# Rotary tables turned once and repeated through DRAM, a parity mask spread by loads: one change to a hybrid decoder block

## Chip, core and metric

The kernel runs on one core of a Trainium2 chip. The metric is the device time of one execution in microseconds; the figure that counts is the median over several runs of the whole kernel.

## What is computed

The reference is a decoder block on 1024 positions of width 1024, in float32. Two of its parts matter here: the rotary embedding of q and k, and the masked attention of three head groups.

```python
def apply_partial_rope(t, cos, sin):          # first 16 of 64 dims of each head
    t1, t2 = rot[..., :half], rot[..., half:] # half = 8
    rotated = concatenate([t1 * cos - t2 * sin, t1 * sin + t2 * cos])

def reference(x, positions, ...):
    inv_freq = ROPE_THETA ** (-arange(0, ROT_DIM, 2) / ROT_DIM)   # 8 frequencies
    ang = positions[..., None] * inv_freq                         # 1024 x 8
    cos, sin = cos(ang), sin(ang)
    h = rms_norm(x, mix_norm_g)
    z_a, q, k, v, gate_logits = split(h @ w_in)
    y_a = chunked_spatial_gating(gelu(z_a), ...)
    q, k = apply_partial_rope(q, cos, sin), apply_partial_rope(k, cos, sin)
    y_b = dilated_mixture_attention(q, k, v)   # groups (128,1), (512,4), (2048,16)
    merged = sigmoid(g_A) * (y_a @ w_branch_a) + sigmoid(g_B) * (y_b @ w_branch_b)
    x = x + merged @ w_out
    ...                                        # norm, convolutional gated MLP, final norm
```

The third attention group, number 2, has dilation 16. The kernel handles it in eight tiles of 128 positions that interleave two residues, so a query may see a key only if both have the same parity in the tile and the key is not later: its mask is a parity mask with a causal one on top.

## The kernel before

**Tiles and order.** All big products are float32 products split in high and low parts, with the transposed activations as moving operand and weights as stationary one. The stage in which the change lies is the input projection `h @ w_in`. It goes by pairs of 256 output columns; each pair is seven products P1 to P7 (a Strassen-like scheme), and each product is 12 matmuls of 128x128 by 128x512 into one PSUM bank (`in_product`, L534). The list `in_order` (L327) fixes the order; the loop over it (L1385) has index i. Pairs 0 and 1 are done ahead; pair 2 is the last of the zv columns, pairs 3, 4, 5 are q/k (rotated dims), q/k (other dims) and v of attention group 1, pairs 6 to 8 the same of group 2, 9 to 11 of group 0. Index i = 7 ends pair 2, i = 8 to 13 are the rest of pair 3, i = 14 to 20 pair 4, i = 21 on pair 5.

**Who sets the order.** TensorE (PE) runs in program order throughout. VectorE (DVE) and ScalarE (ACT) run in program order up to i = 18 (`ordered`, L1379 to L1400); from then on, and for SyncE (SP, which issues nearly all DMAs) and GpSimd (POOL) everywhere, a planner at build time orders each engine's instructions by when it thinks that their inputs are there. On the chip each engine then takes its own list strictly in order. An instruction written later in the program but free to move can be placed between ordered ones.

**Work hung on the matmuls.** After each sixth matmul of a product `tick()` (L216) runs; `after(n, fn)` puts fn on the n-th tick from now, so two ticks are one product. Beside i = 13 to 20 run `norm_v` and `spatial(b)`, b = 0 to 7, one `spatial` at the end of each of these products (L713): 24 small matmuls into two PSUM tiles `pm`, then six passes on DVE (L738) that read them, then stores to DRAM (`mixd`, L743). Both `pm` tiles come from `ps_tr`, a pool of two banks (`tr_tile`, L154). `in_ahead(i, 9, 4)` (L334) loads weights nine places ahead into five buffers `wr` and splits operands four places ahead (ACT L313 the high part, DVE L314 the low one). `sums_ahead` makes the sums that two of the operands need (DVE L278 to L280).

**The rotary tables.** `rot_tables` (L2459) works in `lent`, the part of a buffer `swap` that is free until the first q/k pair is ready. A chain of small DVE steps reduces the angles of 128 positions by 64 (8 blocks of positions by 8 frequencies); `sines` (L2513) makes the two 128x64 tables `sn` and `cs` on ACT. The rotation needs them the other way round, in `YC`: two tables of 128 rows by 1024 positions, where the rows repeat the 8 frequencies four times for each of four heads, with the sign of half the sine rows turned. To get there, `widen` (L2519, 16 ACT passes of 128x128, at i = 12, 13 and 14 in `meanwhile`, L1309) repeats columns into `YC`, and `turn` (L2533, four calls at i = 15 to 18) turns four 128x128 blocks each on PE into a bank of the pool `ps_x` and copies them back into `YC` on ACT (L2538).

**The rotation.** At the end of i = 13 `turned` (L775) gets the buffer `swap` again, loads into it the two halves of the pair's tile C crosswise (L781), and 12 ticks later, at the end of i = 19, `rope` (L783) does for two halves of the positions: `swap *= sin` (L794), `C *= cos` (L795), `C += swap` (L796). Groups 2 and 0 read the same tables later.

**The masks.** `open_attention` (L1072, during pair 5) builds the masks. For group 2, `parity_mask` (L1097) multiplies a row `sign` of alternating +1 and -1 by itself on PE into a `ps_tr` bank `pg`, DVE turns that into 0 or -1e30 (L1100, the trace names the tile `mask`), POOL makes it causal (L1092). Its reader is `score` (L856) of group 2, many products later.

Of the kernel before, what the change touches and what calls it, by code (L numbers as in the profile page):

```python
# [20 lines left out]
P = 128  # L21
# [73 lines left out]
def block_kernel(  # L95
# [58 lines left out]
    def tr_tile(name):  # L154
        return ps_tr.tile([P, HALF], F32, name=name, tag="tr")
# [646 lines left out]

    scratch = {g: dram.tile([S, SW], F32, name=f"scr{g}") for g in (1, 2)}
    summed_d = {g: dram.tile([256, S], F32, name=f"od{g}") for g in (1, 2)}
    share_d = dram.tile([3 * NH, S], F32, name="share")

    def by_channel(t):
# [264 lines left out]
    def open_attention():  # L1072


        nonlocal at, kring, mask, mask2, stats
        at = at_stack.enter_context(tc.tile_pool(name="at", bufs=2, reuse_waits="tile"))
        kring = at.tile([P, KSLOTS, 2, NH, P], F32R, name="kring", bufs=1)
        mask = at.tile([P, 3 * P], F32, name="mask", bufs=1)
        mask2 = at.tile([P, P], F32, name="mask2", bufs=1)
        stats = at.tile([P, 3, NB, SW], F32, name="stats", bufs=1)  # L1080
        sign = at.tile([P, 2, 256], F32, name="sign", tag="vt", bufs=4)[0:1, 0, 0:P]
        nc.gpsimd.memset(mask, 0.0)
        nc.gpsimd.memset(sign[:, 0::2], 1.0)
        nc.gpsimd.memset(sign[:, 1::2], -1.0)
        for m in (mask[:, 0:P], mask[:, 2 * P : 3 * P]):
            nc.gpsimd.affine_select(
                out=m, in_=m, compare_op=ALU.is_ge, fill=NEG,
                base=0, pattern=[[1, P]], channel_multiplier=-1,
            )

        def causal(m):
            nc.gpsimd.affine_select(  # L1092
                out=m, in_=m, compare_op=ALU.is_ge, fill=NEG,
                base=0, pattern=[[-1, P]], channel_multiplier=1,
            )

        def parity_mask():  # L1097
            pg = tr_tile("pg")
            nc.tensor.matmul(pg[:, :P], sign, sign, start=True, stop=True)
            nc.vector.tensor_scalar(mask2, pg[:, :P], 1.0, -0.5 * NEG, ALU.subtract, ALU.mult)  # L1100
            causal(mask2)

        causal(mask[:, P : 2 * P])
        after(8, parity_mask)

# [72 lines left out]
    at_stack, zv_stack, ya_stack = ExitStack(), ExitStack(), ExitStack()  # L1180
    ps_x_stack = ExitStack()

    rot_halves = []

    def rot_bank(name):
        if not rot_halves:
            t = ps_x.tile([P, 2, HALF], F32, name=name, tag="sc")
            rot_halves.extend((t[:, 1], t[:, 0]))
        return rot_halves.pop()

    def beginning():

        nc.scalar.dma_start(chan, per_channel)
        chain, wide, turns = rot_tables(
            nc, lent, [[YC[:, i, lower], YC[:, i, upper]] for i in range(2)],
            rot_bank, ident, pos, YC,
        )

        def some(n):
            for _ in range(min(n, len(chain))):  # L1200
                chain.pop(0)()

        halves, first, then = (slice(0, 256), slice(256, HALF)), range(4), range(4, 8)
        nc.scalar.activation(gate, mhalf, AF.Gelu)
        warm_up(9)
        both(lead_parts(0, halves[0]), raw_left(0, 0, 1), lead_parts(0, halves[1]))
        for cs in halves:
            lead_step(first, 0, cs)
        for kt in range(1, QK):
            both(raw_left(0, kt, 1))  # L1210
            both(lead_parts(kt))
            lead_step(first, kt)
        some(3)
        both(raw_left(0, 4), lead_parts(4))
        some(3)
        both(lead_parts(5))
        some(9)
        lead_step(first, 4)
        lead_step(first, 5)
        for b in range(4):  # L1220
            square_row(0, b)
        load_rows(1, range(2, 4))
        load_x(1, range(2, KT))
        root(0)
        both(raw_left(0, 6, 1), lead_parts(6))
        diagonal(0)
        both(raw_left(0, 7, 1), lead_parts(7))
        for p in range(3):
            if p == 1:
                bc0 = spread(0)  # L1230
            for b in first:
                lead_pass(b, 6, p)
        h1_hi, h1_lo = raw_left(1, 0)
        h1_hi()
        for b in first:
            lead_step((b,), KT - 1)
        for b in range(3):
            square_row(1, b)
        lead_final(0)
        square_row(1, 3)  # L1240
        lead_final(1)
        root(1)
        h1_lo()
        for kt in range(KT):
            scale_x(0, kt, bc0)
        diagonal(1)
        both(raw_left(1, 2))
        both(raw_left(1, 4), raw_left(1, 6))
        lead_step((4, 5), 0)
        lead_step((4, 5), 1)  # L1250
        lead_step((6, 7), 0)
        bc1 = spread(1)
        lead_step((6, 7), 1)
        lead_step(then, 2)
        lead_step(then, 3)
        a11, a12 = left_of("A11"), left_of("A12")
        for hi, _ in a11:
            hi()
        for k in range(2):
            for kt in (2 * k, 2 * k + 1):  # L1260
                scale_x(1, kt, bc1)
                scale_x(1, kt + QK, bc1)
            x_sum(1, k)
            x_sum_dma(3, k)
        lead_final(2)
        lead_final(3)
        for _, lo in a11:
            lo()
        for hi, _ in a12:
            hi()  # L1270
        in_ahead(0, 9, 1)
        x_sum(2, 0)
        lead_step(then, 4)
        lead_step(then, 5)
        for _, lo in a12:
            lo()
        in_ahead(0, 9, 2)
        s2 = left_of("S2")
        square_lead(first)
        s2[0][0]()  # L1280
        lead_step(then, 6)
        in_sums(FIRST, "P6")
        p6 = in_split(FIRST, "P6")
        in_ready["op"] += 1
        x_sum(2, 1)
        in_product(FIRST, "P1")
        p6[0]()
        p6[1]()
        s2[0][1]()
        s2[1][0]()  # L1290
        s2[1][1]()
        in_sums(FIRST, "P4")
        for b in then:
            lead_step((b,), KT - 1)
        s3 = left_of("S3")
        for hi, _ in s3:
            hi()
        a22 = left_of("A22")
        for k in range(2):
            x_sum_dma(4, k)  # L1300
        return some, lambda: len(chain), wide, turns, a22, s3

    late = {}

# [4 lines left out]
    def meanwhile(i):  # L1309
# [48 lines left out]
        elif i in (7, 8, 9, 10):  # L1358
            if i == 7:
                late[FIRST + 1, "P6"][1]()  # L1360
                in_ahead(i, 9, 4)
                in_sums(FIRST + 1, "P4")
            some(5 if i > 7 else 4)
        elif i == 11:
            some(steps_left() - 1)
        elif i == 12:
            some(99)
            for fn in wide[:4]:
                fn()
        elif i == 13:  # L1370
            for fn in wide[4:10]:
                fn()
        elif i == 14:
            for fn in wide[10:]:
                fn()
        elif i in (15, 16, 17, 18):
            turns.pop(0)()

    ordered = ExitStack()  # L1379
    ordered.enter_context(  # L1380
        tc.manual_schedule(engines={mybir.EngineType.DVE, mybir.EngineType.Activation})
    )
    some, steps_left, wide, turns, a22, s3 = beginning()
    WD_START = in_order.index((NP_IN - 3, "P6"))
    for i, (n, name) in enumerate(in_order):  # L1385
        in_ahead(i, 9, 4 if i > 7 else 0)
# [1069 lines left out]
    return rs  # L2456


def rot_tables(nc, lent, wides, bank, ident, pos, out):  # L2459

# [7 lines left out]
    s0, s1 = s[:, 0:W], s[:, W:]  # L2470
    lim = 0.49999995
    two_pi = float(np.float32(2 * np.pi))
    steps, spreads = [], []

    def step(fn, *args):
        steps.append(lambda: fn(*args))
# [6 lines left out]
    for i, f in enumerate(INV_FREQ):  # L2483
# [1 line left out]
    step(nc.vector.tensor_copy, posT, pos)  # L2485
    step(
        nc.vector.tensor_tensor,
        ang.rearrange("p (t f) -> p t f", f=NF),
        posT.unsqueeze(2).to_broadcast([P, NB, NF]),
        freq.unsqueeze(1).to_broadcast([P, NB, NF]),  # L2490
        ALU.mult,
# [24 lines left out]

    steps.append(sines)

    def widen(i, c, rep):  # L2519
        nc.scalar.activation(  # L2520
            wides[i][c].rearrange("p (b r f h) -> p r b f h", b=4, r=4, h=NH)[:, rep],
            (cs, sn)[i][:, 4 * c * NF : 4 * (c + 1) * NF].rearrange("p (b f) -> p b f", b=4)
            .unsqueeze(3).to_broadcast([P, 4, NF, NH]),
            AF.Copy,
            scale=-1.0 if i == 1 and rep < 2 else 1.0,
        )

    for i in range(2):
        for c in range(2):
            for rep in range(4):  # L2530
                spreads.append(lambda i=i, c=c, rep=rep: widen(i, c, rep))

    def turn(i, c):  # L2533
        pt = bank(f"rot_{i}_{c}")
        for k in range(4):
            ks = slice(k * P, (k + 1) * P)
            nc.tensor.transpose(pt[:, ks], wides[i][c][:, ks], ident)
        nc.scalar.activation(out[:, i, c * HALF : (c + 1) * HALF], pt, AF.Copy)  # L2538

    turns = [lambda i=i, c=c: turn(i, c) for i in range(2) for c in range(2)]  # L2540
    return steps, spreads, turns


def tiled(w, cols):
# [50 lines left out]
```

## Time and profile before

| | |
|---|---|
| median of 3 runs | 1343.32 us (1343.31 to 1344.57) |
| the profiled execution | 1342.83 us, of which the profile's span is 1341.0 us |
| granted TensorE clock | 0.999 of full |
| DVE, ACT, POOL busy | 1037.5, 648.4, 283.9 us |
| DMA | 240.19 MB, mean 179 GB/s |

Times in the profile are microseconds from the start of the span. In a list of instructions in order of time, the columns are start, duration, engine, line, operation, written tile `<-` read tiles, shapes and how many instructions were merged into the row; in brackets stands how long the engine was idle before, and what ended that. PE is a matmul, PEld the load of its stationary operand, SPq the issue of a DMA. The durations of matmuls overlap, since they are pipelined: what a group of them costs is read from the start of what follows. In the list of DMA issues the last column is the median time from issue to landing.

### The profile page before, as it was taken

The numbers are of one execution on the slowest core, as the hardware profiler recorded it, in microseconds if no ns is written. First come the engines' busy times: TensorE is split into PE (matmuls) and PEld (weight loads), VectorE is DVE, ScalarE is ACT, GpSimd is POOL, SyncE is SP. The second block draws the span as 40 slices with busy tenths as digits, with TensorE's granted clock in tenths as the row PEclk, the third lists the DMA queues.
The fourth block names the chain that finished last, engine by engine and source line by source line (L and its number), as shares of the span: only waits on it lengthen the run. The fifth ranks groups of instructions, "written<-read, shape, count | busy, mean of one in ns | idle before, by whom it ended". The sixth has DMA issues, their size and how long they took to land.

```text
span 1341.0 us, 19015 instructions
## 1 busy us (share of the span) xinstructions
PE 1332.4 (99%) x6405; PEld 1100.5 (82%) x6405; DVE 1037.5 (77%) x1808; ACT 648.4 (48%) x1267; POOL 283.9 (21%) x270
## 2 busy tenths in 40 slices
PE   9999999999999999999999999999999999999997
PEld 8888888888888888888888888888888888888886
DVE  7989696886768957759789789777777778576675
ACT  7762566666633325245365333433343335454453
POOL 1121000000000000120010337656565653000002
PEclk9999999999999999999999999999999999999999
DMA  9436444545439733975650324444445538986663
GB/s 353 108 98 186 118 139 132 159 148 168 130 107 273 272 108 121 300 254 189 198 178 17 126 97 154 166 165 165 163 151 173 175 123 293 396 313 222 197 205 126
DMA packets 148305, 240.19 MB, mean 179 GB/s; under 512 B 18320, under 2 KB 58864, under 8 KB 148208
## 3 DMA queue, kind: packets, MB, share of 16 engines
q1 hardware_dynamic: 145968, 234.99, 53.6%
q0 software_dynamic: 1088, 2.10, 0.9%
q10 hardware_dynamic: 1152, 1.89, 0.4%
q8 instruction: 51, 0.84, 0.3%
q14 instruction: 46, 0.38, 0.1%
HBM read 170.91 MB, written 64.34 MB: 175 GB/s over the span
## 4 chain that ended last, share of the span: by engine, by line
PE 98%; DVE 1%; ACT 0%; issue 0%; POOL 0%; POOLq 0%; DVEq 0%; ACTq 0%
PE in_P L545 30%; PE uP L2016 21%; PE dn L2298 15%; PE up L2016 9%; PE wo_P L1847 5%; PE pa L1477 5%; PE pl L618 3%; PE pu L1996 2%; PE pb L1477 2%; PE pu L935 1%; PE pp L916 1%; PE pm L733 1%; PE sc L865 1%; PE ht L1751 1%; PE sc L869 0%; PE avt L971 0%
## 5 line engine op out<-in xcount | busy, mean ns | idle before, releaser
L545 PE MATMUL in_P<-R,G 128*128 128x512 f32 x1008 | 237.3, 391 | 0.0
L545 PEld LDWEIGHTS in_P<-R,G 128*128 128x128 f32 x1008 | 187.4, 188 | 38.8 <-issue 0.3
L2298 PE MATMUL dn<-R 128*128 128x512 f32 x924 | 209.6, 389 | 0.0
L2298 PEld LDWEIGHTS dn<-R 128*128 128x128 f32 x924 | 173.4, 188 | 36.0
L170 ACT ACTIVATE R<-up 128x512 fp32r<-128x512 f32 x109 | 65.8, 623 | 122.9 <-DVE up L280 105.6
L2016 PE MATMUL uP<-G,R 128*128 128x512 f32 x504 | 121.4, 389 | 0.0
L2016 PE MATMUL uP<-R 128*128 128x512 f32 x504 | 121.1, 389 | 0.0
L313 ACT ACTIVATE G<-wr 128x512 fp32r<-128x512 f32 x126 | 78.4, 628 | 88.1 <-PE in_P L545 61.2
L2016 PE MATMUL up<-G,R 128*128 128x512 f32 x504 | 120.3, 389 | 0.0
L545 PE MATMUL in_P<-G,G 128*128 128x512 f32 x504 | 119.9, 391 | 0.0
L314 DVE TENSOR_TENSOR G<-wr,G 128x512 fp32r<-128x512 f32 x126 | 86.7, 689 | 42.7 <-ACT G L313 41.8
L2016 PEld LDWEIGHTS uP<-G,R 128*128 128x128 f32 x504 | 94.4, 188 | 20.2 <-issue 0.4
L2016 PEld LDWEIGHTS up<-G,R 128*128 128x128 f32 x504 | 94.6, 188 | 19.7
L2016 PEld LDWEIGHTS uP<-R 128*128 128x128 f32 x504 | 94.6, 188 | 19.6
L545 PEld LDWEIGHTS in_P<-G,G 128*128 128x128 f32 x504 | 93.7, 188 | 19.6 <-issue 0.3
L171 POOL TENSOR_TENSOR G<-wbs,G 128x512 fp32r<-128x512 f32 x12 | 17.0, 1432 | 437.9 <-ACT G L170 437.9
L171 POOL TENSOR_TENSOR R<-up,R 128x512 fp32r<-128x512 f32 x55 | 79.4, 1456 | 13.4 <-ACT R L170 12.1
L170 ACT ACTIVATE R<-db 128x512 fp32r<-128x512 f32 x77 | 48.0, 625 | 53.4 <-PE dn L2298 43.8
L171 DVE TENSOR_TENSOR R<-db,R 128x512 fp32r<-128x512 f32 x77 | 53.6, 700 | 24.9 <-ACT R L170 24.8
L1477 PE MATMUL pa<-R,G 128*128 128x512 f32 x288 | 67.9, 389 | 0.0
L1477 PEld LDWEIGHTS pa<-R,G 128*128 128x128 f32 x288 | 54.1, 188 | 11.2
L545 PE MATMUL in_P<-G 128*128 128x512 f32 x252 | 61.5, 391 | 0.0
(303 smaller groups left out, 2355.3 us busy)
## 6 DMA issues: line engine op xcount, KB each, us to landing
up<-in_w_up_dram SPq DMA_DIRECT2D x44, 512.0 KB, 4.1
wr<-in_w_in_dram SPq DMA_DIRECT2D x42, 512.0 KB, 4.1
dA<-gd SPq DMA_DIRECT2D x55, 256.0 KB, 4.7
dS<-gS SPq DMA_DIRECT2D x44, 256.0 KB, 4.5
db<-wT SPq DMA_DIRECT2D x44, 256.0 KB, 4.5
gd<-Y SPq DMA_DIRECT2D x42, 256.0 KB, 2.0
db<-in_w_down_dram SPq DMA_DIRECT2D x33, 256.0 KB, 4.9
gated<-C SPq DMA_DIRECT2D x32, 256.0 KB, 2.4
```

The source lines that it names most:

```text
L170: nc.scalar.activation(hi, src, AF.Copy)
L171: fn = lambda: lo_eng.tensor_tensor(lo, src, f32(hi), ALU.subtract)
L313: lambda: nc.scalar.activation(op[:, 0], src, AF.Copy),
L314: lambda: nc.vector.tensor_tensor(op[:, 1], src, f32(op[:, 0]), ALU.subtract),
L545: nc.tensor.matmul(acc, op[:, w, kt, :], left[LEFT[name], kt][:, a, :], start=opened and i == 0, stop=i == len(HIGH_FIRST) - 1, skip_group ...
L618: nc.tensor.matmul(lead_banks[b][:, cs], raw_x[h, kt][:, a, c * P : (c + 1) * P], lead_op(kt, w, cs), start=kt == 0 and p == 0 and cs.star ...
L733: nc.tensor.matmul(acc[hs], v[:, hs], wspT[:, (c * 2 + s) // 3, :], start=True, stop=True)
L1477: nc.tensor.matmul(acc, unit[a][kt // 4][:, kt % 4, :], two(R, 8 * h + kt)[:, b, :], start=n == 0 and i == 0, stop=n == len(kts) - 1 and i ...
L1847: nc.tensor.matmul(acc, left[LEFT[name], kt][:, a, blk * P : (blk + 1) * P], out_ops[s][:, w, :], start=name not in SHARED and kt == 0 and ...
L1996: nc.tensor.matmul(acc, plain_up[which, k][:, w, kt, :], left[f"A{h + 1}{k + 1}", kt][:, a, :], start=n == 0 and i == 0, stop=n == KT - 1 ...
L2016: nc.tensor.matmul(acc, op[w][:, kt, :], left[LEFT[name], kt][:, a, :], start=opened and i == 0, stop=i == len(HIGH_FIRST) - 1, skip_group ...
L2298: nc.tensor.matmul(accs[blk], dops[s][:, 0, a, blk * P : (blk + 1) * P], dops[s][:, 1, w, :], start=SEQ[j] not in CONTINUES and kt == 0 an ...
```

## The change

Three things are edited. **The tables:** the angles are laid out by frequency and then block, not block and then frequency. `widen` is gone. One `turn` on PE turns `sn` and `cs` together (they are neighbours in `lent`) into a `ps_tr` bank; two ACT copies bring the turned tables and the negated sines back into `lent`; three DMAs store them as three small tables `rope_d` in DRAM. `repeat` issues eight DMAs from DRAM to DRAM, each of which writes 32 rows of 4 KB (128 KB) of the wide tables `rope_w`, and `load` brings these, 1 MB, into `YC` in one DMA. The three steps stand at i = 13, 14 and 15 instead of the four turns at i = 15 to 18.

**The mask:** POOL writes a stripe of 256 values (two rows of 128 with 0 and -1e30 in turn), one DMA stores it, and two DMAs load its rows into the odd and even partitions of `mask2`. The PE product and the DVE pass are gone. **The causal step** on `mask2` comes six ticks later.

```diff
+    stripe_d = dram.tile([1, 2, P], F32, name="stripe")
...
-        sign = at.tile([P, 2, 256], F32, name="sign", tag="vt", bufs=4)[0:1, 0, 0:P]
+        stripe = at.tile([P, 2, 256], F32, name="stripe", tag="vt", bufs=4)[0:1, 0, 0 : 2 * P]
         nc.gpsimd.memset(mask, 0.0)
-        nc.gpsimd.memset(sign[:, 0::2], 1.0)
-        nc.gpsimd.memset(sign[:, 1::2], -1.0)
+        nc.gpsimd.memset(stripe, 0.0)
+        nc.gpsimd.memset(stripe[:, 1:P:2], NEG)
+        nc.gpsimd.memset(stripe[:, P::2], NEG)
+        nc.sync.dma_start(stripe_d.rearrange("o r t -> o (r t)"), stripe)
...
         def parity_mask():
-            pg = tr_tile("pg")
-            nc.tensor.matmul(pg[:, :P], sign, sign, start=True, stop=True)
-            nc.vector.tensor_scalar(mask2, pg[:, :P], 1.0, -0.5 * NEG, ALU.subtract, ALU.mult)
-            causal(mask2)
+            for r in range(2):
+                nc.sync.dma_start(
+                    mask2[r::2], stripe_d[:, r].partition_broadcast(64).rearrange("q o t -> q (o t)")
+                )
 
         causal(mask[:, P : 2 * P])
         after(8, parity_mask)
+        after(14, lambda: causal(mask2))
...
-    rot_halves = []
-
-    def rot_bank(name):
-        if not rot_halves:
-            t = ps_x.tile([P, 2, HALF], F32, name=name, tag="sc")
-            rot_halves.extend((t[:, 1], t[:, 0]))
-        return rot_halves.pop()
+    rope_d = dram.tile([3, NB * ROT // 2, P], F32, name="rope")
+    rope_w = dram.tile([2, P, S], F32, name="rope_w")
...
-        chain, wide, turns = rot_tables(
-            nc, lent, [[YC[:, i, lower], YC[:, i, upper]] for i in range(2)],
-            rot_bank, ident, pos, YC,
-        )
+        chain, turns = rot_tables(nc, lent, tr_tile, ident, pos, rope_d, rope_w, YC)
...
         elif i == 12:
             some(99)
-            for fn in wide[:4]:
-                fn()
-        elif i == 13:
-            for fn in wide[4:10]:
-                fn()
-        elif i == 14:
-            for fn in wide[10:]:
-                fn()
-        elif i in (15, 16, 17, 18):
+        elif i in (13, 14, 15):
             turns.pop(0)()
...
-        ang.rearrange("p (t f) -> p t f", f=NF),
+        ang.rearrange("p (f t) -> p t f", f=NF),
...
-    def turn(i, c):
-        pt = bank(f"rot_{i}_{c}")
-        for k in range(4):
-            ks = slice(k * P, (k + 1) * P)
-            nc.tensor.transpose(pt[:, ks], wides[i][c][:, ks], ident)
-        nc.scalar.activation(out[:, i, c * HALF : (c + 1) * HALF], pt, AF.Copy)
-
-    turns = [lambda i=i, c=c: turn(i, c) for i in range(2) for c in range(2)]
-    return steps, spreads, turns
+    def turn():
+        pt = bank("rot")
+        nc.tensor.transpose(pt[:, 0:P], lent[:, W : 3 * W], ident)
+        flat, neg = lent[:, 4 * W : 6 * W], lent[0:W, 6 * W : 8 * W]
+        nc.scalar.activation(flat, pt[:, 0:P], AF.Copy)
+        nc.scalar.activation(neg, pt[0:W, 0:P], AF.Copy, scale=-1.0)
+        nc.sync.dma_start(table[1], flat[0:W])
+        nc.sync.dma_start(table[0], flat[W:])
+        nc.sync.dma_start(table[2], neg)
+
+    def repeat():
+        full = wide.rearrange("i (r f h) s -> i r f h s", r=4, f=NF)
+        for i, k, r0, r1 in ((0, 0, 0, 4), (1, 2, 0, 2), (1, 1, 2, 4)):
+            src = table[k].rearrange("(f b) q -> f (b q)", f=NF).unsqueeze(1)
+            for r in range(r0, r1):
+                nc.sync.dma_start(full[i, r], src.to_broadcast([NF, NH, S]))
+
+    def load():
+        nc.sync.dma_start(out, wide.rearrange("i p s -> p i s"))
+
+    turns = [turn, repeat, load]
+    return steps, turns
```

More of the change, by code (lines that the diff above doesn't have):

```diff
@@ L1300, in beginning @@
             x_sum_dma(4, k)
-        return some, lambda: len(chain), wide, turns, a22, s3
+        return some, lambda: len(chain), turns, a22, s3
     late = {}
@@ L1382, in block_kernel @@
     )
-    some, steps_left, wide, turns, a22, s3 = beginning()
+    some, steps_left, turns, a22, s3 = beginning()
     WD_START = in_order.index((NP_IN - 3, "P6"))
@@ L2456, in finish_rms, with rot_tables @@
     return rs
-def rot_tables(nc, lent, wides, bank, ident, pos, out):
+def rot_tables(nc, lent, bank, ident, pos, table, wide, out):
     NF = ROT // 2
@@ L2472, in rot_tables @@
     two_pi = float(np.float32(2 * np.pi))
-    steps, spreads = [], []
+    steps = []
     def step(fn, *args):
@@ L2517, in rot_tables @@
     steps.append(sines)
[L2519 to L2531, printed above, removed]
-    def turn(i, c):
-        pt = bank(f"rot_{i}_{c}")
-        for k in range(4):
-            ks = slice(k * P, (k + 1) * P)
-            nc.tensor.transpose(pt[:, ks], wides[i][c][:, ks], ident)
-        nc.scalar.activation(out[:, i, c * HALF : (c + 1) * HALF], pt, AF.Copy)
-    turns = [lambda i=i, c=c: turn(i, c) for i in range(2) for c in range(2)]
-    return steps, spreads, turns
+    def turn():
[17 more added lines that the diff above has]
+    return steps, turns
 def tiled(w, cols):
```

## The prediction

> **What bounds the kernel now.** I read the page first: share of busy time and chain of work that ended last.
>
> ```profile
> span 1341.0 us, 19015 instructions
> ...
> PE 1332.4 (99%) x6405; PEld 1100.5 (82%) x6405; DVE 1037.5 (77%) x1808; ACT 648.4 (48%) x1267; POOL 283.9 (21%) x270
> ...
> PE 98%; DVE 1%; ACT 0%; issue 0%; POOL 0%; POOLq 0%; DVEq 0%; ACTq 0%
> ```
>
> TensorE is busy for 99% of the span and carries 98% of the last chain. So time taken off PE's list is time off the kernel, as long as PE waits for nothing new, and ACT or DVE passes saved are worth nothing by themselves. Next I asked the waits for the stretch from 90 to 150 us, in which everything that is edited runs.
>
> ```profile
> PEld pm L733 <- issue: 2.8, 8, 0.4
> ...
> PEld in_P L545 <- ACT YC L2520: 0.2, 1, 0.2
> ```
>
> Apart from fixed gaps of the issue, PE waits for another engine once, for 0.2 us. There is no stall here to be removed: the gain is the removed PE work alone, and each new wait is a loss.
>
> **PE work removed.** The list of instructions in order of time, PE alone, shows one product period with a group of turns and one without.
>
> ```profile
> 112.60 3.01 PE L545 MATMUL in_P<-G,G 128*128 128x512 f32 x12
> ...
> 117.00 0.66 PE L2537 MATMUL rot<-ident,YC 128*128 128x128 f32 x4
> 117.41 3.01 PE L545 MATMUL in_P<-G,G 128*128 128x512 f32 x12
> ...
> 120.35 0.66 PE L733 MATMUL pm<-wspT,V 128*64 128x128 f32 x8
> ...
> 121.81 3.06 PE L545 MATMUL in_P<-G 128*128 128x512 f32 x12
> ```
>
> Start to start, the period with turns is 117.41 - 112.60 = 4.81 us, the one without 121.81 - 117.41 = 4.40. Both hold 12 matmuls and one `spatial`. Four turns cost 0.41 us, one about 0.10. Four groups go: 1.64 us; one turn is added: 0.10.
>
> ```profile
> L2537 PE MATMUL rot<-ident,YC x16: 272/273/328, 102.6 to 117.4; 128*128 128x128 f32 x16
> ```
>
> This row gives 273 ns to each turn, but these durations overlap; summed they would be 15 x 0.273 = 4.1 us, and the periods don't show that much. The Trainium skill, "TensorE: Matmul & The Clock Gate", section "Part 4: PE-mode transpose", gives about 275 ns for a 128x128 turn in a kernel's context. As a price of a turn that would be 4.1 us; the periods go against it, the row's duration agrees with it.
>
> For the parity product I use the weight loads:
>
> ```profile
> 126.26 10.79 PEld L545 LDWEIGHTS in_P<-R,G 128*128 128x128 f32 x48 [0.17 <-issue]
> ...
> 137.09 5.40 PEld L545 LDWEIGHTS in_P<-G,G 128*128 128x128 f32 x24
> ...
> 142.84 0.29 PEld L1099 LDWEIGHTS pg<-sign 1*128 1x128 f32 x2 [0.35 <-issue]
> ...
> 145.91 6.76 PEld L545 LDWEIGHTS in_P<-R,G 128*128 128x128 f32 x30
> ```
>
> Undisturbed, 48 loads take 137.09 - 126.26 = 10.83 us, 0.226 each. From 137.09 to 145.91 stand 36, which would be 8.12; it takes 8.82, so `pg` costs 0.70 us. PE saves 1.64 - 0.10 + 0.70 = 2.24 us.
>
> **The new turn and its bank.** The turn moves from i = 15 to i = 13, straight behind the first `spatial`, and from a bank of its own pool to `ps_tr`, whose two banks then hold the two `pm` tiles just written. PE runs in program order, so it stands until DVE has emptied one.
>
> ```profile
> 92.34 0.24 ACT L2515 ACTIVATE ones<-ones 128x64 f32<-128x64 f32 x1
> ...
> 92.61 0.91 ACT L2520 ACTIVATE YC<-ones 128x128 f32<-128x128 f32 x4
> 92.67 1.04 PE L733 MATMUL pm<-wspT,C 128*64 128x128 f32 x16
> ...
> 93.43 0.62 ACT L313 ACTIVATE G<-wr 128x512 fp32r<-128x512 f32 x1
> ...
> 93.64 3.06 PE L545 MATMUL in_P<-R,G 128*128 128x512 f32 x12
> ...
> 94.08 0.69 DVE L314 TENSOR_TENSOR G<-wr,G 128x512 fp32r<-128x512 f32 x1 [1.62 <-ACT G L313]
> ...
> 95.34 0.60 DVE L738 SCALAR_TENSOR_TENSOR V<-pm,chan,b_bc 128x128 f32<-128x128 f32 x2
> ...
> 95.87 1.12 DVE L738 SCALAR_TENSOR_TENSOR C<-pm,chan,b_bc 128x128 f32<-128x128 f32 x4
> ```
>
> Today PE goes on at 93.64 with i = 14, while the first `pm` tile (two passes, written `V`) is read until 95.34 + 0.60 = 95.94. The chain before those passes gets shorter: DVE waits for ACT's L313, which stands behind four `widen` passes that go. L313 would start at 92.61, not 93.43, and the passes end 0.82 earlier, at 95.12. PE then stands from 93.64 to about 95.15: **1.5 us**. Bounds: nothing, if a bank is free by some other assignment; 2.5, if it is the second tile's (95.87 + 1.12 - 0.82 = 96.17). I take 1.5, since the first tile is written and read first. Behind the waiting turn stand all of i = 14's matmuls. On ACT the two copies wait for the turn in place of six `widen` passes; the operands that are split behind them are wanted four products on. This cost takes back most of the four groups.
>
> **The tables' way through DRAM.** In place of four copies into `YC`, a chain: copies, stores, repeats, load, each waiting for the last to land.
>
> ```profile
> wr<-in_w_in_dram SPq DMA_DIRECT2D x42, 512.0 KB, 4.1
> ...
> q<-qd SPq DMA_DIRECT2D x48, 128.0 KB, 2.9
> ...
> wb<-share SPq DMA_DIRECT2D x24, 128.0 KB, 6.7
> ...
> od<-o SPq DMA_DIRECT2D x2, 1024.0 KB, 4.0
> ...
> own<-in_x_dram SPq DMA_DIRECT2D x1, 1024.0 KB, 8.2
> ...
> scr<-st SPq DMA_DIRECT2D x16, 4.0 KB, 1.9
> ```
>
> ```profile
> L1045 SPq DMA_DIRECT2D wb<-share x24: 444/541/777, 395.6 to 430.1; - x24
> ```
>
> Turn at 95.15 and two small copies (0.24 each, as the sine above): about 95.9. Three stores, 0.54 each to issue, 1.9 to land: 99.4. Eight repeats, 4.3 to issue, the last landing 2.9 (plain 128 KB) to 6.7 (the broadcast one) later: 106.6 to 110.4. The load of 1 MB, 4.0 to 8.2: **110.6 to 118.6**, in the middle 114.6. No transfer from DRAM to DRAM stands in the trace; these rows bound it from the sides.
>
> ```profile
> 98.98 1.96 SPq L781 DMA_DIRECT2D swap<-C  x2
> ...
> 107.49 1.12 DVE L738 SCALAR_TENSOR_TENSOR C<-pm,chan,b_bc 128x128 f32<-128x128 f32 x4 [0.26 <-PE pm L733]
> ...
> 108.53 1.08 DVE L795 TENSOR_TENSOR C<-C,YC 128x512 f32<-128x512 f32 x1
> ...
> 110.72 0.66 PE L733 MATMUL pm<-wspT,V 128*64 128x128 f32 x8
> ...
> 119.11 1.12 DVE L738 SCALAR_TENSOR_TENSOR C<-pm,chan,b_bc 128x128 f32<-128x128 f32 x4
> ...
> 122.97 2.05 DVE L794 TENSOR_TENSOR swap<-swap,YC 128x512 f32<-128x512 f32 x2
> ...
> 126.14 0.68 DVE L585 TENSOR_TENSOR C<-C,in_P 128x512 f32<-128x512 f32 x1
> ```
>
> In program order `rope` is due at 122.97, 4 us behind even the late end: the chain itself is hidden. `swap`'s loads, which now wait for the stores out of `lent` and not for the last `widen`, move from 98.98 to about 99.4 or some us later, and have the same cover. But today the two cosine multiplies (L795, about 1.1 each) were slipped in early, at 108.53 and shortly after, because half of the table was there. With one load for all they come late and push L585 by 2.2, from an end of 126.82 to 129.0. L585 frees the bank of the product that starts 12 matmuls after 126.26, at 128.97. That costs about **0.1 us** (nothing to 2.2).
>
> **The rest at nothing.** The stripe's three memsets, its store and two loads of 64 KB: POOL is at 21%, and the mask is read by group 2 alone, whose attention starts after pair 8, more than a dozen products later; if that cover were gone, it would cost about the broadcast row's 6.7. SP gets 12 issues for the tables and 3 for the mask, some 8 us in all; what is queued behind them is a rival below. The ACT passes that go were covered by PE and give nothing back.
>
> **The sum.** -2.24 + 1.5 + 0.1 = -0.64 us against the profiled execution's 1342.83: 1342.19. The median of the runs is 0.49 above that execution, so on its scale 1342.7. About 0.2% (2.7 us) is what a measurement of this kernel can tell from no change; I forecast no change, chance 0.40.
>
> **Rivals.**
>
> *DVE stands before the tables* (slower). The planner places by when it thinks that data is there. If it thinks the load landed near the place where L795 stands now, 108.5, DVE's list holds a multiply there which on the chip waits until 114.6: 6 us, with the `pm` passes behind it. PE wants those banks soon: the passes ending at 107.49 + 1.12 = 108.61 were wanted at 110.72, so 2.1 us are hidden and 3.9 lost: 1346.6. It decides from 2.1 us of waiting and passes 0.2% from 5.4. With a landing at 118.6 it is 1350.7. For it: L795 did run ahead of its place, and a chain of three transfers adds up errors. Against: the waits show DVE standing before a DMA seldom. Chance 0.20.
>
> *The repeats at half rate* (slower).
>
> ```profile
> 102.97:107.78 4.81, 4.81 (x43) 3.85 (x42) 3.68 (x12) 2.11 (x5) 1.18 (x3) 1.00 1.02 275
> ```
>
> With all DMA engines busy (share 1.02) they move 275 GB/s, so 1 MB takes 3.8 us; on half of the engines 7.6, and the load lands 3.8 later, at 118.4. Before 122.97 that costs nothing; with a multiply waiting early it makes the rival above 1350.5. Chance 0.05. The Trainium skill, "DMA: Bandwidth & Descriptors", section "Why a DMA increments its semaphore by 16 and not by 1", says that a transfer runs on the largest number up to 16 that divides the slowest dimension of both sides, which is 8 for these repeats. No row here shows a transfer of that shape.
>
> *Weights come late.*
>
> ```profile
> 110.24 0.34 SPq L270 DMA_DIRECT2D wr<-in_w_in_dram  x1
> ...
> 114.64 0.69 DVE L278 TENSOR_TENSOR wt<-wr 128x512 f32<-128x512 f32 x1
> ```
>
> Issued at 110.24, landed 4.1 later (the first row of the DMA issues above), about 114.3, used at 114.64: nothing to spare. If SP's list has the 1 MB load ahead of it, it lands up to 3.8 later, DVE stands, and the `pm` passes that end at 119.11 + 1.12 = 120.23 for a product wanting them at 120.35 are late too. Half of that, 2, gives 1344.7, still no change. Chance 0.13.
>
> *No bank wait:* -2.14, so 1341.2. Chance 0.15. *Each turn worth its full 273 ns* (faster): -4.1 - 0.70 + 1.6 = -3.2, so 1340.1. The periods speak against it. Chance 0.05. *Nothing gained, since the second `pm` bank is waited for:* +0.4, so 1343.7; 0.02.
>
> **The numbers.** Faster by over 0.2% is the full-price rival, 0.05; slower are the first two, 0.25; the others, 0.40 + 0.13 + 0.15 + 0.02 = 0.70, lie within. The range from 1341.0 to 1347.5 leaves out the full-price case and the upper part of the slower ones, some 0.18 together; the likeliest case alone, with its bounds, is 1341.1 to 1345.8.
>
> **What the profile after would show.** One `rot` of one matmul between `pm` and i = 14, with PE idle some 1.5 us before it, released by DVE L738; no `pg`; periods from i = 15 to 18 of 4.40. L795 behind the load, which lands at 110 to 119, and no DVE wait for `YC`. A wait of DVE on the DMA into `YC`, or of L278 on `wr`, longer than 5 us would prove me wrong, as would periods that stay at 4.8.

## The result, and the profile after

The changed kernel takes 1349.00 us (median of 7 runs, 1348.24 to 1349.40), the kernel before beside it 1343.98 (7 runs, 1343.14 to 1345.08). The ratio is 1.0040 [1.0031, 1.0050]: slower by 0.4%, where no change was forecast, and above the range's end of 1347.5. The profiled execution of after took 1348.48 us, that of before 1342.83.

First the page of after: span, busy time, chain of work that ended last.

```profile
span 1346.7 us, 18978 instructions
...
PE 1331.8 (99%) x6388; PEld 1099.3 (82%) x6388; DVE 1037.9 (77%) x1807; ACT 644.3 (48%) x1249; POOL 281.0 (21%) x271
...
PE 95%; DVE 3%; ACT 1%; issue 1%; POOL 0%; POOLq 0%; DVEq 0%; ACTq 0%
```

PE has 17 matmuls less and 0.6 us less to do, yet the span is 5.7 us longer. The chain says where to look: PE's share falls from 98% to 95%, DVE and ACT now carry 4%. The waits of PE over the whole span (us in total, times, longest) name the places; before, the stretch from 90 to 150 us had one wait of 0.2 us.

```profile
PE in_P L545 <- ACT G L313: 3.2, 1, 3.2
...
PE rot L2509 <- DVE V L738: 1.4, 1, 1.4
PE in_P L545 <- ACT C L573: 1.3, 1, 1.3
```

Only the middle one, the bank wait, was forecast. To price all of them I set the two lists of PE side by side, matmul by matmul (both kernels do the same products), with the difference of the starts set to 0 at i = 12. It grows so (the zero takes out 0.44 us by which after is ahead at that place):

| place | after minus before, us |
|---|---|
| new turn and its bank, ahead of i = 14 | +1.49 |
| four groups of turns gone, i = 14 to 18 | -1.59 |
| a `spatial` near i = 19, not followed up | +0.34 |
| i = 23 (pair 5, P2) | +1.41 |
| to the old place of `pg` | +0.14 |
| `pg` gone | -0.66 |
| **i = 29 (pair 6, P6)** | **+5.17** |
| the rest of the kernel | -0.26 |
| sum | +6.04 |

Next the list of after in order of time, at the turn, one period, the tables, and the two late waits.

```profile
93.88 0.60 DVE L738 SCALAR_TENSOR_TENSOR V<-pm,chan,b_bc 128x128 f32<-128x128 f32 x2
...
94.63 0.30 PE L2509 MATMUL rot<-ident,ones 128*128 128x128 f32 x1 [1.36 <-DVE V L738]
94.68 3.01 PE L545 MATMUL in_P<-R,G 128*128 128x512 f32 x12
...
103.53 3.06 PE L545 MATMUL in_P<-R,G 128*128 128x512 f32 x12
...
107.97 3.06 PE L545 MATMUL in_P<-R,G 128*128 128x512 f32 x12
...
111.95 0.36 SPq L2525 DMA_DIRECT2D YC<-rope_w  x1
...
129.20 0.63 ACT L313 ACTIVATE G<-wr 128x512 fp32r<-128x512 f32 x1 [3.87 <-PE in_P L545]
...
131.92 0.63 ACT L313 ACTIVATE G<-wr 128x512 fp32r<-128x512 f32 x1 [2.09 <-PE in_P L545]
132.45 0.58 ACT L573 ACTIVATE C<-in_P 128x512 f32<-128x512 f32 x1
...
133.09 5.73 PE L545 MATMUL in_P<-R,G 128*128 128x512 f32 x24 [1.25 <-ACT C L573]
133.78 1.07 DVE L794 TENSOR_TENSOR swap<-swap,YC 128x512 f32<-128x512 f32 x1
...
139.16 0.34 SPq L798 DMA_DIRECT2D qd<-C  x1
...
141.92 2.29 SPq L270 DMA_DIRECT2D wr<-in_w_in_dram  x2
...
147.68 0.69 DVE L278 TENSOR_TENSOR wt<-wr 128x512 f32<-128x512 f32 x1
...
149.73 0.60 ACT L573 ACTIVATE C<-in_P 128x512 f32<-128x512 f32 x1 [4.81 <-PE in_P L545]
...
151.49 0.68 DVE L280 TENSOR_TENSOR wr<-wr 128x512 f32<-128x512 f32 x1
...
152.21 0.63 ACT L313 ACTIVATE G<-wr 128x512 fp32r<-128x512 f32 x1 [0.84 <-DVE wr L280]
...
152.89 6.07 PE L545 MATMUL in_P<-R,G 128*128 128x512 f32 x18 [3.19 <-ACT G L313]
```

And the same view of before, for the instructions that moved most.

```profile
105.20 0.57 SPq L270 DMA_DIRECT2D wr<-in_w_in_dram  x1
...
126.25 0.34 SPq L798 DMA_DIRECT2D qd<-C  x1
...
129.35 0.60 ACT L573 ACTIVATE C<-in_P 128x512 f32<-128x512 f32 x1 [3.82 <-PE in_P L545]
```

The turn at 94.63 with its 1.36 us before it, and the period of 107.97 - 103.53 = 4.44 us (4.81 before), are as forecast. The load into `YC` is issued at 111.95, 1.6 us later than the latest that the prediction reckoned (110.4). From there on the lists differ. The rotation (L794) starts at 133.78 and not at 122.97, in DVE's list behind the work of three more products; its row has no wait, so it ran as soon as DVE came to it. Its result is stored by SP (L798) at 139.16 and not 126.25. Behind these stores stands, in SP's list, the load of the second half of pair 6's weights: first of the two at 141.92, where before it was issued at 105.20, ahead of the rotation. SP's own waits from 90 to 150 us show that it stood idle ahead of the stores, for the last step of the rotation (L796), with this load behind them:

```profile
SPq L798 <- DVE C L796: 10.3, 1, 10.3
```

The operand for i = 29 needs it: sums at 147.68 and 151.49, split at 152.21, PE at 152.89 after standing 3.19. ACT adds its part: its list has the splits behind the eviction of i = 28 (149.73, after 4.81 us of waiting for PE), so PE waits for ACT, which had waited for PE. At i = 23 the same in small: two splits, each waiting for PE to free an operand buffer, stand ahead of the eviction L573, which ran at 129.35 before and at 132.45 now; i = 23 adds into the bank that it reads.

The theory: neither the transfers nor their real lateness cost these 6.6 us, but the order that the planner at build time wrote down. The rival: the new traffic, the 12 issues on SP and the hop over DRAM are really late or in the way. A second rival: the weights' place in SP's list alone.

### The profile page after: what moved, and what is told of

Read it like the earlier page. It is cut to its first block, busy times and chain, and to the rows that moved or that the text cites. A ratio compares the mean times of both kernels' runs of the same rounds, so it can differ in the third digit from the quotient of the medians.

```text
span 1346.7 us, 18978 instructions
## 1 busy us (share of the span) xinstructions
PE 1331.8 (99%) x6388; PEld 1099.3 (82%) x6388; DVE 1037.9 (77%) x1807; ACT 644.3 (48%) x1249; POOL 281.0 (21%) x271
## 4 chain that ended last, share of the span: by engine, by line
PE 95%; DVE 3%; ACT 1%; issue 1%; POOL 0%; POOLq 0%; DVEq 0%; ACTq 0%
PE in_P L545 29%; PE uP L2004 20%; PE dn L2286 15%; PE up L2004 8%; PE wo_P L1835 5%; PE pa L1465 5%; PE pl L618 3%; PE pu L1984 2%; PE pb L1465 2%; PE pu L936 1%; PE pp L917 1%; PE sc L866 1%; PE pm L733 1%; PE ht L1739 1%; PE sc L870 0%
## 5 line engine op out<-in xcount | busy, mean ns | idle before, releaser
L171 POOL TENSOR_TENSOR G<-wbs,G 128x512 fp32r<-128x512 f32 x12 | 17.0, 1436 | 434.1 <-PE in_P L545 383.4
L171 POOL TENSOR_TENSOR R<-up,R 128x512 fp32r<-128x512 f32 x55 | 79.3, 1454 | 13.3 <-ACT R L170 12.2
L171 DVE TENSOR_TENSOR R<-db,R 128x512 fp32r<-128x512 f32 x77 | 53.8, 702 | 24.9 <-ACT R L170 24.8
```

What stands on the lines that cost most here:

```text
L171: fn = lambda: lo_eng.tensor_tensor(lo, src, f32(hi), ALU.subtract)
```

## The experiments

Where a table of starts is spoken of, it is made as above: difference to before, 0 at i = 12.

**The mask alone.** Into the kernel before, only the mask's part of the change:

```diff
-            pg = tr_tile("pg")
-            nc.tensor.matmul(pg[:, :P], sign, sign, start=True, stop=True)
...
+            for r in range(2):
+                nc.sync.dma_start(
+                    mask2[r::2], stripe_d[:, r].partition_broadcast(64).rearrange("q o t -> q (o t)")
+                )
...
+        after(14, lambda: causal(mask2))
```

> The kernel before with the mask's part of the change alone. Lists theory (the 5 us are lost where the planner's lists put weight loads and an eviction late because of the tables): the parity product costs PE 0.70 us and goes, the rest is hidden, so 0.5 to 0.8 us under the kernel before. Rival, the stripe's DMAs disturb the start of the first attention group: 1 to 3 us above it, with a wait of PE between 140 and 165 us.

Measured: 1341.99 us (11 runs) beside 1343.29 (28 runs), ratio 0.9990 [0.9982, 0.9999]. By the starts -0.66 at the old place of `pg`, and -0.54 about 500 us later, at the tile `wo_P`, a step that after has as well. The kernel with idle copies, below, has nothing of the mask's part and yet the same -0.54 there, so that step is not the mask's. The mask's part is a small gain; the loss is in the tables.

**Weights called earlier.** In the kernel after, the loads are issued 13 places ahead, not 9, while i is 13 to 20:

```diff
-        in_ahead(i, 9, 4 if i > 7 else 0)
+        in_ahead(i, 13 if 13 <= i <= 20 else 9, 4 if i > 7 else 0)
```

> The changed kernel, with the weight loads of places 13 to 20 asked for 13 places ahead and not 9, so that the load for the P6 of pair 6 stands in the program before the rotation. Lists theory: SP's list has that load ahead of the rotation's stores, the wait of 4.1 us at i = 29 goes, and 1344.5 to 1345.5 is left (bank wait 1.4 and late eviction 1.3 stay). Rival, the extra traffic through DRAM makes data late: the transfers are all still there, so within 1 us of the changed kernel, 1348 to 1349.5.

Measured: 1347.22 us (6 runs), ratio 1.0036 [1.0023, 1.0048]: a miss, 1.7 us above the range. PE's waits in its trace, from 90 to 175 us:

```profile
PE sc L870 <- DVE kring L171: 1.9, 1, 1.9
PE rot L2509 <- DVE V L738: 1.5, 1, 1.5
PE in_P L545 <- ACT C L573: 1.3, 1, 1.3
```

The wait at i = 29 is gone, so the late load was needed for it. But the rotation is as late as in after, its stores too, and now the first attention scores (L870) wait for the split of a k (L171) that is stored, loaded and split after them: +2.21 by the starts. The late weights were one symptom; the late rotation is what has to be explained.

**No wide table.** The eight repeats go from the small tables straight into `YC`; the load is gone:

```diff
-                nc.sync.dma_start(full[i, r], src.to_broadcast([NF, NH, S]))
+                nc.sync.dma_start(out[32 * r : 32 * r + 32, i, :], src.to_broadcast([NF, NH, S]))
...
-        nc.sync.dma_start(out, wide.rearrange("i p s -> p i s"))
+        pass
```

> The changed kernel, but the eight repeats go from the small tables in DRAM straight into YC, and the wide table in DRAM and its load are gone: one hop and 2 MB of traffic less, as many DMA issues but one. Lists theory: the rotation is planned some us earlier, the weight loads stand before its stores and the P1 eviction before the two splits again, both PE waits go: 1342.8 to 1343.6 (only the bank wait of 1.4 left of the losses). Traffic rival: the same direction, but in steps with bytes, so still 2 us or more above the kernel before, as two thirds of the bytes are left. If the broadcast loads themselves are slow, the rotation waits for YC and it stays above 1346.

Measured: 1343.44 us (11 runs), ratio 1.0003 [0.9994, 1.0011]. Both late waits are gone (0.00 at i = 23 and at i = 29). What is left is the bank wait (+1.63) and 1.24 at a later `spatial`, which the next kernel shows. This fits the theory and the rival of a really late chain alike, since both the transfer and the planner's idea of it are gone.

**No wide table, and a bank of its own.** As the last, and the turn takes its bank from `ps_x`, as the old turns did:

```diff
-        chain, turns = rot_tables(nc, lent, tr_tile, ident, pos, rope_d, rope_w, YC)
+        def own_bank(name):
+            return ps_x.tile([P, 2, HALF], F32, name=name, tag="sc")[:, 0]
+
+        chain, turns = rot_tables(nc, lent, own_bank, ident, pos, rope_d, rope_w, YC)
```

> As the run without the wide table, and the turn gets a bank of the pool ps_x, as before the change, and not one of the two that the spatial step uses. If the wait for the bank costs what the prediction's working gave it, PE loses its 1.4 us wait before the turn: 1341.5 to 1342.2, 1.2 to 1.6 under the run without the wide table, and about 2 us under the kernel before. Rival: DVE, which is busy nearly all of that time, makes PE wait somewhat later instead, and no more than 0.5 us is gained.

Measured: 1341.73 us (11 runs), ratio 0.9990 [0.9981, 0.9998]. The bank wait is gone, +0.08 in place of +1.63. In its list in order of time one cost is left:

```profile
116.73 1.08 DVE L795 TENSOR_TENSOR C<-C,YC 128x512 f32<-128x512 f32 x1
...
119.00 0.60 DVE L738 SCALAR_TENSOR_TENSOR V<-pm,chan,b_bc 128x128 f32<-128x128 f32 x2
...
119.74 0.66 PE L733 MATMUL pm<-wspT,V 128*64 128x128 f32 x8 [0.54 <-DVE V L738]
```

Here the planner slips a cosine multiply in early, ahead of the passes that empty the `pm` banks, and PE loses 1.23 us over the next `spatial`. The planner errs on either side.

**Only the lists.** The kernel after with every transfer, the wide table and the bank kept. DVE and ACT stay in program order up to i = 22 (the same constant lets `sums_ahead` run up to there, which takes in one more sum, that for P4 of pair 5):

```diff
-    ORDERED = 18
+    ORDERED = 22
```

> The kernel after with all its transfers, the wide table in DRAM and the hop over it kept; only VectorE's and ScalarE's lists are held in program order up to i = 22 and not 18. Theory of the build-time lists: the two late waits of the kernel after (1.41 at i = 23 and 5.17 at i = 29) came from where the planner put things, since it took the load of the tables for late; with the rotation held in its program place both go, and the wait for the new turn's bank (1.5) stays: 1349.0 - 6.6 = 1342.4, within 1342.0 to 1343.5. Rival, the traffic or the real lateness of the tables: the transfers are all still there, so the time stays at 1347 or above, and VectorE stands before the tables on the chip.

Measured: 1342.21 us (11 runs) beside 1343.10 (27 runs), ratio 0.9995 [0.9986, 1.0004]. Its list in order of time:

```profile
112.67 0.36 SPq L2525 DMA_DIRECT2D YC<-rope_w  x1
...
122.65 1.07 DVE L794 TENSOR_TENSOR swap<-swap,YC 128x512 f32<-128x512 f32 x1
...
123.77 0.43 SPq L270 DMA_DIRECT2D wr<-in_w_in_dram  x1
...
128.17 0.34 SPq L798 DMA_DIRECT2D qd<-C  x1
...
129.03 0.60 ACT L573 ACTIVATE C<-in_P 128x512 f32<-128x512 f32 x1 [3.82 <-PE in_P L545]
```

This decides it. The transfers are those of after and go out at the same places, the first store at 95.44 (in after 95.27) and the load into `YC` 0.7 us later than in after, yet L794 runs at 122.65, again with no wait: the tables were there. The weight load stands ahead of the rotation's stores, L573 in its old place, both late waits are gone, and so is the 0.34 at the `spatial` near i = 19; of the losses only the bank wait remains. By the starts the difference behind i = 29 is -0.53, where the prediction's sum was -0.64.

**The turn's own bank alone.** The kernel after with nothing but the edit of the bank shown above.

> The kernel after, with nothing changed but the bank of the new turn, which comes from the pool that the four old turns used. Theory: the 1.4 to 1.5 us that TensorE stands before the turn go and nothing else moves: 1347.5, within 1347.2 to 1348.0, both late waits still there. Rival: TensorE is held at that place by VectorE's passes anyway, one product later, so that the wait only moves: 1349, no change.

Measured: 1348.88 us (5 runs) beside 1343.10, ratio 1.0039 [1.0027, 1.0052]. The median shows no gain, yet the list in order of time shows the wait at the turn gone (its last row is i = 29):

```profile
93.36 0.33 PE L2512 MATMUL rot<-ident,ones 128*128 128x128 f32 x1
93.44 3.01 PE L545 MATMUL in_P<-R,G 128*128 128x512 f32 x12
...
151.65 7.06 PE L545 MATMUL in_P<-R,G 128*128 128x512 f32 x18 [3.19 <-ACT G L313]
```

By the starts the 1.41 us are gained at the turn and kept up to i = 29. There the loss is 6.16 and not 5.17. The table by stretch (stretch, length, PE busy, granted clock, DMA share, GB/s) says why. First this kernel:

```profile
150.00:151.00 1.00, 0.00 (x0) 0.79 0.48 140
151.00:152.00 1.00, 0.35 (x1) 0.50 0.67 194
...
156.00:157.00 1.00, 1.00 (x4) 0.50 0.47 137
157.00:158.00 1.00, 1.00 (x5) 0.80 0.44 125
```

Then the kernel after:

```profile
152.00:153.00 1.00, 0.11 (x1) 1.00 0.69 199
153.00:154.00 1.00, 1.00 (x4) 0.82 1.17 228
154.00:155.00 1.00, 1.00 (x3) 0.50 0.73 266
...
156.00:157.00 1.00, 1.00 (x4) 0.50 0.04 16
157.00:158.00 1.00, 1.00 (x6) 0.97 0.32 94
```

At the long stall the granted clock falls to half: in after for about 0.18/0.5 + 3 + 0.03/0.5 = 3.4 us, here for about 0.21/0.5 + 6 + 0.2/0.5 = 6.8. So the 5.17 of after are two things, 3.35 of standing and 1.82 behind it, where the matmuls are slow (the lost clock, 0.18 + 3 x 0.5 + 0.03, gives 1.71); here they are 3.35 and 2.81. From there to the end after gains 0.26 and this kernel loses 0.43, which I didn't follow up. The stated rival, that the wait only moves, is right for the median and wrong for the mechanism. The interval holds the forecast of 1347.5 as well; by this run alone the bank's worth stays open.

**Idle copies in the kernel before.** Three stores, eight repeats and a copy of 1 MB of the same sizes, which nobody reads (the stores take a constant tile, the copy ends in DRAM), stand in the program at i = 13, 14 and 15:

```diff
+    def ghost(i):
+        if i == 13:
+            for k in range(3):
+                nc.sync.dma_start(rope_d[k], ident[0:64])
+        elif i == 14:
...
+                    nc.sync.dma_start(full[j, r], src.to_broadcast([ROT // 2, NH, S]))
+        elif i == 15:
+            nc.sync.dma_start(
+                rope_x.rearrange("i p s -> p i s"), rope_w.rearrange("i p s -> p i s")
+            )
```

> The kernel before with its own tables as they are, and beside them three stores, eight repeats and one 1 MB copy of the same sizes at i = 13, 14 and 15, issued by SyncE, each waiting for the one ahead; what they move is read by nobody (the last goes from DRAM to DRAM, since there is no free room for it). Theory of the lists: traffic, issues and SyncE's waits cost nothing by themselves, since no reader is placed by them: 1343.3 to 1344.2, within 0.1% of before. Rival, traffic: some of the 5 to 6 us lost by the kernel after shows here, 1346 or more, as TensorE waiting for operands whose weights were loaded late.

Measured: 1343.93 us (11 runs) beside 1343.10, ratio 1.0006 [0.9998, 1.0015]. By the starts +0.20 behind i = 29, with no step above 0.15 up to there. But the planner, which orders SP's list, did not leave the copies where the program has them:

```profile
30.73 1.79 SPq L1190 DMA_DIRECT2D rope<-ident  x3
...
38.60 5.19 SPq L1196 DMA_DIRECT2D rope_w<-rope  x5
...
83.62 1.39 SPq L1196 DMA_DIRECT2D rope_w<-rope  x2
...
105.64 0.71 SPq L1198 DMA_DIRECT2D rope_x<-rope_w  x1
```

The stores and the repeats were issued before the stretch in question, and of the twelve only the copy of 1 MB lies in it. So this run shows that the copy there, and the others at their places, cost some tenths in the profile (by the medians up to 2 us, the end of the interval). It does not try the stores and repeats beside i = 13 and 14. For those the rival of traffic falls by the kernel listed to 22, which has all twelve transfers between 95.44 and 112.67 and neither late wait.

**No wide table, own bank, listed to 22.** The fourth kernel with `ORDERED = 22`.

> Repeats straight into the tables (no wide table, no last load), the turn's own bank, and VectorE's and ScalarE's lists in program order up to i = 22. The version with the first two alone lost 1.23 us where a cosine multiply stood ahead of the passes that read the pm banks; held in program order it can't. Theory: 1341.7 - 1.2 = 1340.5, within 1340.0 to 1341.0, which is 0.2% below the kernel before. Rival: the 1.23 is paid at another place, where the multiply then stands: 1341.7.

Measured: 1340.54 us (11 runs), ratio 0.9980 [0.9972, 0.9989]. The multiply of 116.73 stands behind L794 again, and the 1.23 us are gone (by the starts +0.05).

**The kernel before, listed to 22.** The control for that constant: before, with `ORDERED = 22` and nothing else.

> The kernel before with nothing changed but VectorE's and ScalarE's lists held in program order up to i = 22. Theory: the kernel before lost nothing to the planner, so this gives nothing: 1343.1, within 0.1%; then what the listed versions of the kernel after gain against before is the change's own gain. Rival: the longer ordered stretch is a gain by itself: 1342.3 or below.

Measured: 1343.29 us (11 runs) beside 1343.39 (21 runs), ratio 1.0002 [0.9993, 1.0011]. The longer ordered stretch gives the kernel before nothing.

**Listed to 22, own bank, wide table kept.** The kernel after with both edits.

> The kernel after with the lists held to i = 22 (as in e5) and the new turn in its own bank (as in e6); wide table, hop and all transfers kept. In e6 the gain of the bank, 1.4 at its place, was eaten at i = 29, where the granted clock after the long stall stayed at half for 6.6 us and not 3.4. Theory: with no stall at i = 29 there is nothing to eat it: 1.4 to 1.5 below e5, 1340.7 (1340.2 to 1341.2). Rival: the bank's wait only moves to a later place: 1342.2, as e5.

Measured: 1340.45 us (11 runs) beside 1343.39, ratio 0.9980 [0.9971, 0.9989]. By the starts the difference behind i = 29 is -1.93, where the fifth kernel had -0.53: the bank's wait was worth its 1.40 where no stall follows; by the medians, each taken against the kernel before beside it, it is about 2. In the profiled execution, at 1341.56 the longest of the eleven, some 2 us are lost again later, 1.3 of them at 215 us, where PE waits for DVE (L902); whether this is in the other executions too, one trace doesn't tell. With all transfers of the change in place this is 0.2% below the kernel before (0.1 to 0.3% by the interval) and further below after, and it matches the version without the wide table: the hop through DRAM costs nothing that these runs can tell.

**After once more.** The kernel after unchanged.

> The kernel after, unchanged, profiled a second time. Question: the half clock after the stall at i = 29 lasted 3.4 us in the first profile and 6.6 us in that of e6. If its length is a matter of chance, it can come out at either here, and the span with it (1346.7, or 1 to 2 us more); if it belongs to the program, it is 3.4 us again. The stall itself, 3.2 us, must be there in any case; the median is expected at 1348.5 to 1349.5.

Measured: 1349.38 us (4 runs, 1347.10 to 1350.59), ratio 1.0046 [1.0032, 1.0060]. The profiled execution is the shortest, 1347.10. The same table by stretch:

```profile
152.00:153.00 1.00, 0.00 (x0) 1.00 0.68 199
153.00:154.00 1.00, 0.89 (x4) 1.00 1.09 237
154.00:155.00 1.00, 0.96 (x5) 1.00 0.88 360
```

The stall is the same, 3.19 us and 3.36 by the starts; the clock does not fall this time, and the rest of the step is 0.47 and not 1.82. These 1.35 us are about the 1.38 by which this execution is shorter than the first profiled one. So 0.47 of the 1.82 does not hang on the clock. The stall belongs to the program, the half clock behind it comes and goes.

## Why the prediction was wrong

**PE work removed: right.** Forecast 1.64 for the four groups and 0.70 for `pg`; measured 1.59 and 0.66. A turn in the stream cost 0.10 us, not the 273 ns of its row; the full-price rival falls.

**The bank: right.** Forecast 1.5, and 0.10 for the turn; measured 1.49 for both together, and the wait goes with a bank of the turn's own. The rivals of no wait and of the second bank fall.

**The cosine multiplies: right in size.** Forecast 0.1 (nothing to 2.2); with the rotation in its program place (fifth kernel) no step above 0.2 appears there.

**The chain through DRAM: hidden on the chip, as forecast.** The load was issued at 111.95, a little later than the latest reckoned; in the kernel listed to 22 it went out at 112.67, and the tables were in use at 122.65 with no wait.

**The step that failed** is the sentence "In program order `rope` is due at 122.97, 4 us behind even the late end: the chain itself is hidden", and with it "The rest at nothing", as far as it covers what is queued on SP. `rope` is not in program order: i = 19 lies behind `ORDERED = 18`, where the planner sets the lists. The chain was hidden on the chip but, as far as the lists show, not in the planner's reckoning. It put the rotation 10.8 us later (133.78 for 122.97), and what it then ordered around the rotation made PE wait twice: a weight load stood behind the rotation's stores, 36.7 us later than before, and ACT's evictions behind splits. The sum of the two late waits is 6.6 us, of which 1.8 came behind the standing at i = 29, about 1.4 of them by the slow clock. The lists alone, put back, took 1349.00 to 1342.21 beside a before of 1343.10: -0.89 by the medians and -0.53 by the starts behind i = 29, where -0.64 was forecast.

**The rivals.** "DVE stands before the tables" had the planner's error in view and the wrong sign: it took the planner for too early, and DVE never stood. "Weights come late" (0.13) named the mechanism in part, with the wrong load and price. It let the load of 110.24 feed the sum of 114.64; that sum belongs to an earlier pair whose weights had been there for long, and the load to pair 7. The load that decided was the one of 105.20, which had some 20 us to spare in before (issued 105.20, its first sum at 131.71) and lost them in SP's list. The price of half of 3.8 us was taken from the transfer's length, when a place in the list could cost any amount. "The repeats at half rate" decided nothing: the load, which waits for the last repeat, went out 4.3 us after that repeat's issue (107.64 to 111.95), within the 2.9 to 6.7 that the working took, and no multiply stood before the tables. On how many DMA engines the repeats ran, no row tells.

None of the signs that the prediction named for being wrong appeared: DVE did not wait for `YC`, L278 did not wait for `wr`, and the periods came down to 4.44. No sign asked whether the rotation would run at its place.

What stays open: that the planner overrates this chain is argued from the lists (one hop less moves the rotation forward, holding it in order costs no wait); its own estimate stands in no trace.

## What to carry to other kernels

Where a planner writes each engine's list, ask of a change not only when its data is there on the chip, but what the planner will believe, and which loads and evictions stand in the lists behind the consumer that it moves. Before blaming traffic, put the lists back with everything else kept: that one kernel told list and transfer apart here. A control whose copies the planner is free to move has to be looked up in its trace: here most of them ran elsewhere. A gain of 1.4 us on the critical engine can be invisible as long as a later stall and the clock behind it vary by as much.

## What the hardware showed that was not expected

A stall of TensorE can cost more than its length. At the one of 3.2 us the granted clock fell to 0.50 in two of three profiles, for 3.4 and 6.8 us, and 1.8 and 2.8 us more were lost behind it; in the third it did not fall, and 0.5 us was lost. At the stalls of 1.3 us (i = 23, in the same three profiles) and 1.9 us (weights called earlier, one profile) it stayed at 1.00. The Trainium skill, "TensorE: Matmul & The Clock Gate", section "Part 1: The HAM clock gate (the "warmup" mystery)", says that the clock goes to half after an idle window of about 3.4 us, comes back after as much sustained work, and that the window runs freely, so that it varies from run to run. The halving, its length in one profile (twice that in the other) and the variation agree; but a stall a little shorter than that window was enough twice. In the kernel with the turn's own bank the clock fell some 2.1 us after PE had stopped: PE stood from 151.65 - 3.19 = 148.46, and the 0.79 granted from 150 to 151 puts the fall at about 150.6. Here the measurement decides: less idle time than the page's window was enough.
